# A GLA and retention trunk on one core: values and gates of a retention head as a pair, with seven block products for half their k-tiles

## The chip, the core and the metric

The kernel runs on one core of a Trainium2 chip. The core has TensorE (PE, matrix products into PSUM), VectorE (DVE), ScalarE (ACT), GpSimd (POOL) and SyncE (SP), and 16 DMA engines that SP, ACT and POOL feed through queues. The metric is the device time of one execution in microseconds, as the median of several runs. "PEld" in the profile is the loading of the stationary operand of a matmul, which overlaps the matmuls.

## The reference

Two layers with a residual each, then an RMS norm. The first is gated linear attention (GLA, 4 heads), the second retention (8 heads); both project a normalised input of 256 tokens x 2048 to queries, keys, values and gates, and project 4096 gated outputs back. The retention layer, which the change is about, in short:

```
proj = h @ w_in                                  # h: 256 x 2048
q, k, v, gate = split(proj)                      # per head 256, 256, 512, 512 columns
q, k = rotary(q), rotary(k)
o = (q k^T * decay, causal) v                    # per head
o = (o - mean(o)) * rsqrt(var(o) + EPS) * gn_g + gn_b
h = h + (o * silu(gate)) @ w_out
```

All arrays are float32.

## The kernel before

**Precision.** A float32 operand is split in two parts, hi and lo = x - hi, both of type float32r, and a product is three matmuls: hi·hi, hi·lo and lo·hi. The activations are split once (`xhl` for the layer's input, `ogt` for the gated outputs; 16 k-tiles of 128 rows, 2 parts, 256 tokens). The weights stream from HBM and are split on the way: ScalarE copies a piece to hi (L152), VectorE subtracts to get lo (L153).

**Groups and pieces.** All weights lie in one array, in the order of use, in groups of 2048 x 512. A group is 16 k-tiles; a load (`emit_raw`, L119, SP's queue) brings 4 k-tiles (1 MB), a split piece is 2 k-tiles (128 x 1024). There are three buffers for loads and three for hi and lo; pieces are split up to two ahead of TensorE (`LOOK`). `group_x` (matmuls at L189 to L191 in `mm3`) gives 2 token halves x 512 columns: per piece 12 matmuls of 512 columns. `group_w` (L229 to L233) gives the transposed queries and keys in four PSUM banks.

**A retention head** (`ret_head`) takes three groups: queries and keys (`rqk`), values (`rv`), gates (`rg`). While TensorE runs the `rv` group, `ret_scores` applies the rotation (L812 to L817), splits q and k, multiplies them and the decay table, and splits the scores. In the `rg` group `o_part` multiplies scores and values, takes mean and variance with the batch statistics instructions (L868, L869) and normalises (L870 to L880). The gate product (L890) and the transposes into `ogt` (L459 to L466) run in the next head's `rqk` group. After four heads `out_half` multiplies their 2048 gated columns with `w_out` in four groups and adds to the residual `resid`, which stays in SBUF.

**Order.** These small works are generators in a queue (`side`), of which one step is emitted after each piece; `drain_side` empties it. The tile framework then places each instruction on its engine's queue by priority and by its own estimate of when the inputs are there. Each queue runs in order. SP's queue holds the loads, POOL's the small tables (decay, `gn_g`, `gn_b`).

Of the kernel before, what the change touches and what calls it, by code (L numbers as in the profile page):

```python
# [10 lines left out]
F32 = mybir.dt.float32  # L11
# [6 lines left out]
P = 128  # L18
# [7 lines left out]
CHUNK = 4  # L26
LOOK = 2
DMA_LOOK = 2
# [25 lines left out]

@with_exitstack
def kernel(
# [20 lines left out]
    raw_p = pool("raw", 3)  # L77
    hi_p = pool("hi", 3)
    lo_p = pool("lo", 3)
# [4 lines left out]
    sc_p = pool("sc", 2)  # L84
# [3 lines left out]
    acc_p = pool("acc", 4, space=psum)  # L88
    lev_p = pool("lev", 2, space=psum)
    mis_p = pool("mis", 2, space=psum)  # L90

# [6 lines left out]
    n_groups = w_all.shape[0]  # L98
    raws, splits = {}, {}
    emitted = {"raw": 0, "sub": 0}  # L100
    per_raw = CHUNK // SUB
    raws_per_group = NKT // CHUNK

    last0 = (n_groups - 1) * NSUB

    def emit_raw(parts=1):
        c = emitted["raw"]
        if c >= n_groups * raws_per_group:
            return
        t = raw_p.tile([P, CHUNK, GW], F32, tag="raw", name=f"raw{c}")  # L110
        g, j = divmod(c, raws_per_group)
        src = w_all[g, :, j * CHUNK * GW : (j + 1) * CHUNK * GW].rearrange("p (k n) -> p k n", n=GW)
        step = CHUNK // parts
        raws[c] = t
        emitted["raw"] += 1
# [24 lines left out]
    def emit_split(pieces=1, between=None):  # L140
        i = emitted["sub"]
        if i >= n_groups * NSUB:
            return
        c, j = divmod(i, per_raw)
        while emitted["raw"] <= min(c + DMA_LOOK, n_groups * raws_per_group - 1):
            emit_raw()
        src = raws[c][:, j * SUB : (j + 1) * SUB, :]
# [11 lines left out]
        if j == per_raw - 1:  # L159
            del raws[c]  # L160
        emitted["sub"] += 1

# [16 lines left out]
    def next_weights():  # L179
        i = state["sub"]  # L180
        while emitted["sub"] <= min(i + LOOK, n_groups * NSUB - 1):
            emit_split()
# [10 lines left out]
    def group_x(lhs, name, hook=None, deadline=None, bank=None):  # L193
        bank = bank or (acc_p, "acc")
        ps = [bank[0].tile([P, GW], F32, tag=bank[1], name=f"{name}_ps{t}") for t in range(2)]
        for j in range(NSUB):
# [9 lines left out]
        return ps  # L206

    def group_w(rhs, name, extra=None):
        ps = [acc_p.tile([P, 2, SEQ], F32, tag="acc", name=f"{name}_ps{c}") for c in range(4)]
        for j in range(NSUB):  # L210
# [3 lines left out]
            if last:  # L214
                order = [(q, c) for c in range(4) for q in range(SUB)]
            if j < 3 and extra is not None:
# [28 lines left out]

    def rsqrt(y, m, n, name):
# [17 lines left out]
    resid = const([P, 2, D], "resid")  # L264
# [55 lines left out]
    w0 = emit_raw(4)  # L320
# [3 lines left out]
    w0(2, 2)  # L324
    load_xt(1)(0, 4)
    w1 = emit_raw(2)
    w1(0)
    w1(1)
    load_xt(2)(0, 4)
    emit_raw()  # L330
# [20 lines left out]
    def square_sum(t, c):  # L351
        junk = sg_p.tile([P, GW], F32, tag="sg", name="sqj")
        nc.scalar.activation(
            junk, resid[:, t, c * GW : (c + 1) * GW], AF.Square, accum_out=ssum[:, t, c : c + 1]
# [40 lines left out]
    def gate_low_rank():  # L395
        for t in range(2):
            keep(nc.sync.dma_start(resid[:, t, :], x_n[:, t, :]))
# [42 lines left out]
    def o_mms(sc, v, name):  # L440
        ps = [acc_p.tile([P, GW], F32, tag="acc", name=f"{name}_ps{t}") for t in range(2)]
# [238 lines left out]
    def out_cols(c, ps, t, first, final):  # L680
        dst = resid[:, t, c * GW : (c + 1) * GW]
# [8 lines left out]
    def out_half(first, final, name):  # L690
        for c in range(4):
# [5 lines left out]
            ps = group_x(ogt, f"{name}{c}", deadline=5)  # L697
# [4 lines left out]
            for _ in transpose_out(  # L702
                lambda t, j: resid[:, t, c * GW + j * P : c * GW + (j + 1) * P],
# [16 lines left out]
    def out_tail():  # L720
# [4 lines left out]
        for t in range(2):  # L725
# [3 lines left out]
            ps = [acc_p.tile([P, half], F32, tag="acc", name=f"tail_ps{t}{n}") for n in range(2)]  # L729
# [11 lines left out]
            for n in range(2):  # L741
                dst = resid[:, t, base + n * half : base + (n + 1) * half]
# [8 lines left out]
            for c in (0, 1, 3, 2):  # L751
                src = resid[:, t, c * GW : (c + 1) * GW]
# [53 lines left out]
    def ret_scores(h, box):  # L806
# [207 lines left out]
```

## Time and profile before

| | |
|---|---|
| median of 3 runs | 1416.22 us (1416.16 to 1416.98) |
| profiled execution | 1415.53 us, of it the span 1413.8 us |
| granted TensorE clock | 0.998 |
| busy: PE / DVE / ACT / POOL | 1402.0 / 905.3 / 696.0 / 46.6 us |
| DMA | 266.72 MB, mean 189 GB/s |
| one retention head (start to start of `rqk`) | 70.03 us |

A row by line says: line, engine, operation, output and inputs by the program's names with shape and type, count, then busy time in us and the mean of one in ns, and the idle time of the engine just before, with what ended it. A row of a stretch gives its length and the busy time and count of each engine, the granted clock, the DMA's busy share and GB/s. A row of DMA issues gives count, KB of one and the median us from issue to landing.

### The profile page before, as it was taken

Reading aid. Unit: us, or ns where it says so; the run is one execution under the profiler, and the core shown is the slowest. Engines: PE = TensorE matmul, PEld = TensorE weight load, DVE = VectorE, ACT = ScalarE, POOL = GpSimd, SP = SyncE. Lnnn points to the kernel's source line nnn. Section 1 sums busy time; section 2 is a strip of 40 time slices with the busy share of each in tenths; the row PEclk is TensorE's granted clock in tenths of the full one; section 3 lists DMA queues with packets and bytes.
Section 4 is the critical chain, followed back from the end, with each engine's and each line's share of the span. In section 5 each row is a group of like instructions: output and inputs, shape, how many; then the busy total and the mean of one; then the engine's idle time right before and its main releaser. Section 6 shows DMA issues by size and latency. Waiting matters only on the chain.

```text
span 1413.8 us, 17507 instructions
## 1 busy us (share of the span) xinstructions
PE 1402.0 (99%) x6800; PEld 1179.7 (83%) x6800; DVE 905.3 (64%) x1415; ACT 696.0 (49%) x904; POOL 46.6 (3%) x99
## 2 busy tenths in 40 slices
PE   8999999999999999999999999999999999999997
PEld 7888888888888888888888888888888888888887
DVE  6595795555846774655666666665556666666664
ACT  6665654533555655454444444444344444444453
POOL 1010020000000010000000000000000000000000
PEclk9999999999999999999999999999999999999999
DMA  8654554555555555555555555555555555555662
GB/s 304 242 173 140 208 176 164 195 187 190 177 174 184 182 187 179 179 180 193 193 194 185 199 179 199 181 197 183 204 182 183 197 184 202 180 204 176 207 216 90
DMA packets 40147, 266.72 MB, mean 189 GB/s; under 512 B 4848, under 2 KB 5360, under 8 KB 9344
## 3 DMA queue, kind: packets, MB, share of 16 engines
q1 hardware_dynamic: 36672, 256.92, 53.7%
q0 software_dynamic: 2240, 7.21, 1.5%
q10 hardware_dynamic: 1152, 1.48, 0.3%
q8 instruction: 53, 0.87, 0.2%
q14 instruction: 30, 0.25, 0.0%
HBM read 263.49 MB, written 2.10 MB: 188 GB/s over the span
## 4 chain that ended last, share of the span: by engine, by line
PE 99%; DMA 0%; ACT 0%; DVE 0%; issue 0%; ACTq 0%; DVEq 0%
PE rqk_ps L232 8%; PE gv_ps L189 4%; PE gg_ps L189 4%; PE rv_ps L189 4%; PE gv_ps L191 4%; PE rv_ps L190 4%; PE gg_ps L190 4%; PE gg_ps L191 4%; PE gv_ps L190 4%; PE rv_ps L191 4%; PE rg_ps L189 4%; PE rg_ps L190 4%; PE rg_ps L191 4%; PE rqk_ps L233 4%; PE gqk_ps L232 4%; PE gb_ps L189 2%
## 5 line engine op out<-in xcount | busy, mean ns | idle before, releaser
L153 DVE TENSOR_TENSOR lo<-raw,hi 128x1024 fp32r<-128x1024 f32 (+1 forms) x473 | 576.9, 1222 | 422.1 <-ACT hi L152 421.3
L152 ACT ACTIVATE hi<-raw 128x1024 fp32r<-128x1024 f32 (+1 forms) x473 | 499.3, 1057 | 600.6 <-PE rg_ps L191 104.6
L232 PE MATMUL rqk_ps<-xhl,hi 128*128 128x512 f32 x480 | 166.9, 398 | 0.0
L233 PE MATMUL rqk_ps<-xhl,lo 128*128 128x256 f32 x480 | 126.4, 280 | 0.0
L232 PEld LDWEIGHTS rqk_ps<-xhl,hi 128*128 128x128 f32 x480 | 88.8, 188 | 17.5
L190 PE MATMUL rv_ps<-lo,xhl 128*128 128x512 f32 x256 | 100.4, 392 | 0.0
L190 PE MATMUL gv_ps<-lo,xhl 128*128 128x512 f32 x256 | 100.4, 392 | 0.0
L190 PE MATMUL gg_ps<-lo,xhl 128*128 128x512 f32 x256 | 100.4, 392 | 0.0
L191 PE MATMUL gv_ps<-hi,xhl 128*128 128x512 f32 x256 | 100.2, 392 | 0.0
L191 PE MATMUL gg_ps<-hi,xhl 128*128 128x512 f32 x256 | 100.0, 391 | 0.0
L191 PE MATMUL rv_ps<-hi,xhl 128*128 128x512 f32 x256 | 99.7, 389 | 0.0
L190 PE MATMUL rg_ps<-lo,xhl 128*128 128x512 f32 x256 | 99.6, 389 | 0.0
L191 PE MATMUL rg_ps<-hi,xhl 128*128 128x512 f32 x256 | 99.6, 389 | 0.0
L189 PE MATMUL gv_ps<-hi,xhl 128*128 128x512 f32 x256 | 93.1, 391 | 0.0
L189 PE MATMUL rv_ps<-hi,xhl 128*128 128x512 f32 x256 | 92.1, 390 | 0.0
L233 PEld LDWEIGHTS rqk_ps<-xhl,lo 128*128 128x128 f32 x480 | 89.1, 189 | 3.4
L189 PE MATMUL rg_ps<-hi,xhl 128*128 128x512 f32 x256 | 91.8, 389 | 0.0
L189 PE MATMUL gg_ps<-hi,xhl 128*128 128x512 f32 x256 | 91.7, 391 | 0.0
L232 PE MATMUL gqk_ps<-xhl,hi 128*128 128x512 f32 x216 | 72.7, 397 | 0.0
L191 PEld LDWEIGHTS rv_ps<-hi,xhl 128*128 128x128 f32 x256 | 48.1, 188 | 10.0
L191 PEld LDWEIGHTS rg_ps<-hi,xhl 128*128 128x128 f32 x256 | 48.0, 188 | 10.0
L190 PEld LDWEIGHTS rg_ps<-lo,xhl 128*128 128x128 f32 x256 | 48.1, 188 | 10.0
(273 smaller groups left out, 2402.7 us busy)
## 6 DMA issues: line engine op xcount, KB each, us to landing
raw<-in_w_all SPq DMA_DIRECT2D x238, 1024.0 KB, 4.9
resid<-in_x_n SPq DMA_DIRECT2D x2, 1024.0 KB, 8.1
gg<-in_gn_g POOLq DMA_DIRECT2D x8, 256.0 KB, 3.7
gb<-in_gn_b POOLq DMA_DIRECT2D x8, 256.0 KB, 4.5
raw<-in_w_all SPq DMA_DIRECT2D x3, 512.0 KB, 6.6
xt<-in_x_t SPq DMA_DIRECT2D x3, 512.0 KB, 8.1
dm<-in_dmat POOLq DMA_DIRECT2D x8, 192.0 KB, 2.6
fn<-in_final_norm POOLq DMA_DIRECT2D x4, 256.0 KB, 4.2
```

The lines of the kernel that those rows point to most:

```text
L152: a = nc.scalar.activation(hi[:, sl], src[:, sl], AF.Copy)
L153: b = nc.vector.tensor_tensor(lo[:, sl], src[:, sl], hi[:, sl].bitcast(F32), ALU.subtract)
L189: mm(ps, xh, hi[:, q, :], start=kt == 0, stop=False)
L190: mm(ps, xh, lo[:, q, :], start=False, stop=False)
L191: mm(ps, xl, hi[:, q, :], start=False, stop=kt == NKT - 1)
L232: mm(ps[c], wh, rhs[:, kt, :, :], start=kt == 0, stop=False)
L233: mm(ps[c][:, 0, :], wl, rhs[:, kt, 0, :], start=False, stop=False)
```

## The change

**The pair.** For a retention head write the first 8 k-tiles of the input as four blocks: token halves 1 and 2, k-tiles 0 to 3 (a) and 4 to 7 (b). With the gate weights g and the value weights v, also in halves a and b, the 2 x 2 block product (tokens x {g, v}) takes eight products of 4 k-tiles when written out. The new kernel forms it with seven (`product`), of block sums: X1a·ga, S1·vb, S2·(ga+va), S3·(ga+va+vb), X1b·gb, S4·(va+vb), X2b·(ga+va+vb+gb), where S2 = X2a - X2b or its like are sums of the input blocks (`make_sums`: VectorE and ScalarE once, for all eight heads). K-tiles 8 to 15 go as before (`direct`). A product accumulates in one of the PSUM banks A, B, C, V1, which are partly copied out and partly accumulated on.

**The weight sums.** The pair streams 14 pieces per head from HBM and keeps four of them, x (ga) and z (vb), in their buffers. POOL's queue issues DMAs that add a second piece from HBM onto a buffer (`accum_op`): va onto x, later va onto z and gb onto x. VectorE adds z onto x in place. After each sum the buffer is split again, so the pair takes 22 splits. The order of the pieces is x x, v4, z z, v5, x x, v6, x x, g2 g3, v7, z z, g4, g5, x x, g6, g7 (numbers are pieces of two k-tiles; the doubles serve a product, the others `direct`).

**Streams.** A load is now one piece of 512 KB, into eight buffers assigned ahead (`_plan`); there are four hi and lo buffers, and splits run three pieces ahead.

**The head's rest.** Rotation, scores, outputs and normalisation (`ret_tasks`) now run mostly in the next head: two steps at the head's end, the others in the next `rqk` group and the first pieces of the pair. Mean and variance come from ScalarE's accumulated sums. The `rqk` group uses two of the pair's banks and the two `lev` banks; scores, outputs and transposes share the two `mis` banks. After heads 3 and 7, `out_half` does the first six of eight pieces of its first two groups, beside which the last head's rest runs, and then the last two of each.

**The residual.** `resid` and the sums share one buffer of 16 KB per partition: the residual is stored to HBM (ScalarE's queue) before heads 0 and 4 and loaded in `out_half`; the sums are stored in head 3 and loaded for head 4 (these three from POOL's queue). Heads are counted from 0.

```diff
-CHUNK = 4
-LOOK = 2
-DMA_LOOK = 2
+QK = 4
+LOOK = 3
+DMA_LOOK = 6
+NRAW = 8
...
+    def pair(g, v):
+        x = [load(g, 0), load(g, 1)]
+        for j in range(2):
+            use(x[j], post=[(x[j], (v, j))])
+        plain(v, [4])
+        z = [load(v, 2), load(v, 3)]
+        for j in range(2):
+            use(z[j])
+        plain(v, [5])
+        for j in range(2):
+            use(x[j])
+        plain(v, [6])
+        for j in range(2):
+            use(x[j], pre=z[j], post=[(z[j], (v, j)), (x[j], (g, 2 + j))])
+        plain(g, [2, 3])
+        plain(v, [7])
+        for j in range(2):
+            use(z[j])
+        plain(g, [4, 5])
+        for j in range(2):
+            use(x[j])
+        plain(g, [6, 7])
...
+        for h in range(4 * half, 4 * half + 4):
+            plain(("rqk", h))
+            pair(("rg", h), ("rv", h))
+        out_cols_of("ro", half, CUT)
...
+    def emit_raws(c):
+        while emitted["raw"] < len(loads):
+            n = emitted["raw"]
+            h = held.get(bufs[n])
+            if n > c and (n > c + DMA_LOOK or (h is not None and last_use[h] >= emitted["sub"])):
+                break
+            emit_raw()
...
+        for n in range(i + 1, min(i + 1 + EARLY, len(subs))):
+            at, by = subs[n][:2]
+            if by is not None and n not in added:
+                added.add(n)
+                nc.vector.tensor_tensor(raws[at], raws[at], raws[by], ALU.add)
...
+        for n, key in post:
+            nc.gpsimd.dma_start(raws[n], block(key), accum_op=ALU.add)
+        emit_raws(c)
...
+    def three(ps, xh, xl, hi, lo, q, stop):
+        start, again = id(ps) not in begun, {"skip_group_check": id(ps) in closed}
+        begun.add(id(ps))
+        mm(ps, xh, hi[:, q, :], start=start, stop=False, **again)
+        mm(ps, xh, lo[:, q, :], start=False, stop=False, **again)
+        mm(ps, xl, hi[:, q, :], start=False, stop=stop, **again)
+        if stop:
+            closed.add(id(ps))
+    def product(ps, left, stop=False):
+        for j in range(2):
+            hi, lo = next_weights()
+            for q in range(SUB):
+                k = j * SUB + q
+                three(ps, left(k, 0), left(k, 1), hi, lo, q, stop and k == QK - 1)
+    def direct(lhs, ps, j, stop=False):
+        hi, lo = next_weights()
+        for t in range(2):
+            cols = slice(t * P, (t + 1) * P)
+            for q in range(SUB):
+                kt = j * SUB + q
+                three(ps[t], lhs[:, kt, 0, cols], lhs[:, kt, 1, cols], hi, lo, q, stop and q == SUB - 1)
...
+        s = rs_p.tile([P, 4, QK, 2, P], F32R, tag="rs", name=name)
+        cur["s"] = s
+        tt = nc.vector.tensor_tensor
+        y = [t4_p.tile([P, QK, SEQ], F32, tag="t4", name=f"{name}_y{i}") for i in range(2)]
+        for i in range(2):
+            part = lhs[:, i * QK : (i + 1) * QK].bitcast(F32)
+            tt(y[i], part[:, :, 0, :], part[:, :, 1, :], ALU.add)
+        yield
+        one_, two = slice(0, P), slice(P, SEQ)
+        f = [t4_p.tile([P, 2, QK, P], F32, tag="t4", name=f"{name}_f{i}") for i in range(2)]
+        f3, f5, f6, f7 = f[0][:, 0], f[0][:, 1], f[1][:, 0], f[1][:, 1]
+        tt(f5, y[0][:, :, two], y[1][:, :, two], ALU.subtract)
+        tt(f6, f5, y[0][:, :, one_], ALU.subtract)
+        yield
+        tt(f3, f6, y[1][:, :, one_], ALU.add)
+        tt(f7, y[0][:, :, one_], y[0][:, :, two], ALU.subtract)
+        yield
+        for i, x in ((0, f3), (1, f5), (2, f6), (3, f7)):
+            keep(nc.scalar.activation(s[:, i, :, 0, :], x, AF.Copy))
+            keep(tt(s[:, i, :, 1, :], x, s[:, i, :, 0, :].bitcast(F32), ALU.subtract))
...
+        po = [mis_p.tile([P, GW], F32, tag="mis", name=f"ro{h}_ps{t}") for t in range(2)]
+        o_mms(sc, box["v"], f"ro{h}", po)
+        o = o_p.tile([P, 2, GW], F32, tag="o", name=f"ro{h}")
+        mv = st_p.tile([P, 2, 2], F32, tag="mv", name=f"mv{h}")
+        for t in range(2):
+            nc.scalar.activation(o[:, t, :], po[t], AF.Copy, accum_out=mv[:, 0, t : t + 1])
+        nc.vector.tensor_scalar(mv[:, 0, :], mv[:, 0, :], -1.0 / GW, None, ALU.mult)
+        for t in range(2):
+            mean = mv[:, 0, t : t + 1]
+            nc.scalar.activation(po[t], o[:, t, :], AF.Square, bias=mean, accum_out=mv[:, 1, t : t + 1])
+        yield
+        for t in range(2):
+            keep(nc.vector.scalar_tensor_tensor(o[:, t, :], o[:, t, :], mv[:, 0, t : t + 1], gg, ALU.add, ALU.mult))
...
+        q_ps = [acc(1, f"rqk{h}_ps{c}", (P, 2, SEQ), [c + 2])[0] for c in range(2)]
+        q_ps += [lev_p.tile([P, 2, SEQ], F32, tag="lev", name=f"rqk{h}_ps{c}") for c in (2, 3)]
+        group_w(lhs, f"rqk{h}", lambda j: step() if j < NSUB - 1 else None, q_ps)
...
+        mine = ret_tasks(h, qk, r, r2, {"v": v, "sg": sg})
+        product(A, plain(0, 0), stop=True)
+        step()
+        direct(lhs, (C, V1), 4)
+        copy(sg[:, 0, :], A)
+        step()
+        product(C, summed(0))
+        direct(lhs, (C, V1), 5)
+        while tasks:
+            step()
+        product(B, summed(1), stop=True)
+        direct(lhs, (C, V1), 6)
+        copy(o[:, 1, :], B)
+        begun.discard(id(B))
+        closed.discard(id(B))
+        product(A, summed(2), stop=True)
+        product(B, plain(4, 0))
+        copy(o[:, 0, :], A)
+        direct(lhs, (C, V1), 7, stop=True)
+        tt(o[:, 0, :], o[:, 1, :], o[:, 0, :], ALU.subtract)
+        product(A, summed(3), stop=True)
+        tt(o[:, 0, :], C, o[:, 0, :], ALU.add)
+        copy(sg[:, 1, :], A)
+        direct(lhs, (B, A), 4)
+        v_split(0)
+        tt(o[:, 1, :], o[:, 1, :], sg[:, 1, :], ALU.subtract)
+        direct(lhs, (B, A), 5)
+        tt(o[:, 1, :], V1, o[:, 1, :], ALU.add)
+        product(A, plain(4, 1))
+        v_split(1)
+        tasks.append(mine)
+        direct(lhs, (B, A), 6)
+        step()
+        direct(lhs, (B, A), 7, stop=True)
+        step()
+        for t in range(2):
+            g_done(t)
...
+            if cut and c == 0:
+                if True:
+                    for i in range(2):
+                        pend[i] = acc(2, f"{name}{i}_ps")
+                        steps_x(pend[i], ogt, range(cut), lambda j: hook(i, j))
+                    get_resid(f"{name}_resid")
+                    for i in range(2):
+                        steps_x(pend[i], ogt, range(cut, NSUB))
...
+    put_resid("resid_g")
+    if True:
+        tasks.append(make_sums(xhl, "sums"))
+        for h in range(4):
+            if h == 3:
+                keep_sums("sums")
+            ret_head(h)
+    slots = deque((2, 3, 0, 1))
+    out_half(True, False, "ra", CUT, out_steps)
+    put_resid("resid_r")
+    if True:
+        reload_sums("sums2")
+        for h in range(4, 8):
+            ret_head(h)
+    slots = deque((2, 3, 0, 1))
+    out_half(False, True, "rb", CUT, out_steps)
```

More of the change, by code (lines that the diff above doesn't have):

```diff
@@ L205, in group_x, with group_w @@
             advance()
[L206 to L209 removed]
+    def group_w(rhs, name, extra=None, ps=None):
+        given = ps is not None
+        ps = ps or acc(4, f"{name}_ps", (P, 2, SEQ))
         for j in range(NSUB):
@@ L688, with out_half @@
     fns = {}
-    def out_half(first, final, name):
+    def out_half(first, final, name, cut=0, hook=None):
+        pend = {}
         for c in range(4):
@@ L897, with out_steps @@
+        v_split(1)
[4 more added lines that the diff above has]
+        step()
+        for t in range(2):
+            g_done(t)
+        begun.clear()
+        closed.clear()
+    def out_steps(i, j):
+        step(2 if i == 0 else 1)
     for h in range(2):
```

340 lines of the change are left out of this document (207 added, 133 removed).

## The prediction

> **What bounds the kernel now.** The page comes first (busy time of each engine, chain of work that ended last), then one retention head as a window, then the start times of single matmuls, and last the DMA.
>
> ```profile
> span 1413.8 us, 17507 instructions
> PE 1402.0 (99%) x6800; PEld 1179.7 (83%) x6800; DVE 905.3 (64%) x1415; ACT 696.0 (49%) x904; POOL 46.6 (3%) x99
> PE 99%; DMA 0%; ACT 0%; DVE 0%; issue 0%; ACTq 0%; DVEq 0%
> ```
>
> The chain is TensorE alone. Of the 11.8 us in which it is idle, none lies in a retention head:
>
> ```profile
> core 0: us, PE busy (x) PEld busy (x) DVE busy (x) ACT busy (x) POOL busy (x), PEclk, DMA share, GB/s
> 808.96:878.99 70.03, 70.03 (x349) 59.27 (x348) 46.54 (x67) 31.61 (x40) 1.61 (x3) 1.00 0.57 191
> 808.96:832.20 23.24, 23.24 (x138) 20.38 (x137) 12.97 (x16) 11.22 (x17) 0.00 (x0) 1.00 0.53 181
> 170.00:190.00 20.00, 20.00 (x102) 17.00 (x101) 20.00 (x64) 12.44 (x17) 0.56 (x2) 1.00 0.48 161
> ```
>
> The first row is one whole head (head 2): TensorE 70.03 of 70.03 us. The second is its query/key group. The third is a stretch of a GLA head with VectorE busy for the whole 20 us, and TensorE still without a gap. A busy row can hide waits, because the ends of matmuls are modelled, so the pace is read from starts (start, duration, engine, line):
>
> ```profile
> 832.04 0.39 PE L189 MATMUL rv_ps<-hi,xhl 128*128 128x512 f32 x1
> 832.27 0.39 PE L190 MATMUL rv_ps<-lo,xhl 128*128 128x512 f32 x1
> 832.50 0.39 PE L191 MATMUL rv_ps<-hi,xhl 128*128 128x512 f32 x1
> ...
> 834.77 0.61 PE L189 MATMUL rv_ps<-hi,xhl 128*128 128x512 f32 x2
> ```
>
> The thirteenth starts 834.77 - 832.04 = 2.73 us after the first: 0.227 us each, the same between neighbours, within a bank and across banks. So TensorE is issuing without a gap, and a matmul fewer is 0.227 us less, as long as nothing else comes late.
>
> **What goes.** Before, the first eight k-tiles of values and gates take 8 x 2 token halves x 2 groups x 3 = 96 matmuls of 512 columns per head. Seven products of 4 k-tiles x 3 are 84. The other half (`direct`) keeps its 96; the query/key group, the scores, the outputs and the transposes keep their numbers. 12 matmuls x 0.227 = 2.72 us per head, 21.8 us for eight heads. A head becomes 70.03 - 2.72 = 67.31 us, of which the pair's 180 matmuls are 40.8. This term is certain; all the rest can only add waits, since no other TensorE work goes.
>
> **VectorE and ScalarE.** Rows of head 2, grouped by line (count, then busy us and mean ns):
>
> ```profile
> L153 DVE TENSOR_TENSOR lo<-raw,hi 128x1024 fp32r<-128x1024 f32 x24 | 29.3, 1223 | 18.6 <-ACT hi L152 18.6
> L429 DVE SCALAR_TENSOR_TENSOR rv<-rv_ps,r,rv 128x512 fp32r<-128x512 f32 x2 | 1.4, 751 | 0.4 <-ACT rv L428 0.4
> L868 DVE BATCH_NORM_STATS2 bs<-ro_ps 128x6 f32<-128x512 f32 x2 | 1.4, 700 | 2.5 <-PE ro_ps L450 2.5
> L890 DVE TENSOR_TENSOR ro<-ro,rsg 128x512 f32<-128x512 f32 x2 | 1.4, 692 | 0.4 <-ACT rsg L437 0.4
> L812 DVE TENSOR_TENSOR ra<-rqk,trig 128x1024 f32<-128x1024 f32 x1 | 1.2, 1224 | 0.0
> L813 DVE TENSOR_TENSOR rb<-rqk,trig 128x512 f32<-128x512 f32 x1 | 0.7, 684 | 0.0
> L869 DVE BATCH_NORM_AGGREGATE mv<-bs 128x2 f32<-128x6 f32 x2 | 0.4, 176 | 0.0
> L466 DVE TENSOR_TENSOR ogt<-rot_tp,ogt 128x256 fp32r<-128x256 f32 x4 | 1.6, 416 | 0.0
> ```
>
> The pair splits 22 weight pieces where the two groups split 16, because the x and z pieces are split again after each sum. VectorE: +6 splits x 1.223 = 7.3; +2 adds of 128x1024 as L812, 2.4; +5 combinations of 128x512 as L890, 3.5; +0.2 for the mean; -1.4 and -0.4 for the batch statistics. That is +11.6: 58.2 of 67.3 us, 86%.
>
> ```profile
> L152 ACT ACTIVATE hi<-raw 128x1024 fp32r<-128x1024 f32 x24 | 25.4, 1058 | 33.3 <-PE rg_ps L191 13.1 <-PE rqk_ps L232 9.6 <-PE rv_ps L191 7.7
> L428 ACT ACTIVATE rv<-rv_ps,r 128x512 fp32r<-128x512 f32 x2 | 1.4, 690 | 0.9 <-PE rv_ps L191 0.9
> 837.80 2.35 DVE L153 TENSOR_TENSOR lo<-raw,hi 128x1024 fp32r<-128x1024 f32 x2
> ```
>
> ScalarE: +6 splits x 1.058 = 6.3, +4 PSUM copies and +2 copies and 2 squares of the outputs, 8 x 0.69 = 5.5: 43.4 us, 65%. L152's idle time says that splits now wait for TensorE to free a buffer, so they run as far ahead as the buffers let them.
>
> In the pair alone VectorE has 22 splits (26.9), two adds (2.4), five combinations and two value splits (5.0), rotation L812 and two L813 (2.6), two gate products (1.4) and four of L466 (1.7): 40.0 of 40.8 us as durations. Back to back it is less: two splits take 2.35 us, 1.13 from start to start. A product piece (six matmuls) lasts 1.36 us, so a run of four of them (pieces 10 to 13) can be fed. I cost all this at nothing, covered by TensorE's 40.8 us; the row that bears it out is the window at 170 to 190, VectorE full and TensorE without a gap. If the cover goes, each us of a late split is a us per head, 8 us in all.
>
> One place has little cover. After the sixth product ScalarE copies bank A to sg, and the next direct piece writes B for 1.36 us and then A. A split that has just begun ahead of the copy makes 1.06 + 0.69 = 1.75 us, 0.4 late. Bounds 0 and 0.4 us per head (no gain, a wait only); I take 0.2, because ScalarE is idle for a third of the time.
>
> **The accumulating DMAs.** Six a head, 512 KB each, from POOL's queue. None is in the trace; the nearest rows are plain ones (KB each, us from issue to landing; above them a 2 us slice of a busy stretch):
>
> ```profile
> DMA  9189473039573491780099743692753910891995
> GB/s 385 53 250 391 72 324 143 0 74 406 111 303 164 70 397 57 152 373 0 4 266 307 274 205 98 127 397 33 254 238 66 381 78 0 217 385 61 246 391 84
> raw<-in_w_all SPq DMA_DIRECT2D x14, 1024.0 KB, 4.8
> gg<-in_gn_g POOLq DMA_DIRECT2D x2, 256.0 KB, 3.7
> q1 hardware_dynamic: 36672, 256.92, 53.7%
> mask<-in_mask POOLq DMA_DIRECT2D x1, 256.0 KB, 6.6
> ```
>
> Full slices move about 391 GB/s, so 512 KB are 1.34 us (T) of all engines; gg's 3.7 us less its 0.67 leave 3.0 us fixed on POOL's queue.
>
> When must they land? Take 0 as the start of the pair on TensorE, product pieces 1.36, direct pieces 2.72: piece 7 (x again) starts at 10.9, piece 10 (x with z added) at 16.3, 15 and 16 (z again) at 24.5 and 25.8, 19 (x, the last time) at 32.6. With four buffers the split of piece n starts when piece n-4 ends, and is done 1.06 + 1.22 = 2.3 us later: piece 10's from 10.9 to 13.2. It must start 2.3 us ahead of its matmuls at the latest. The first accumulates (v into x) thus have from about -6.0 (splits start three query/key pieces ahead) to 8.6: 14.6 us. The last (g into x) have 13.2 to 30.3. Tightest is the second z: from 13.2 to 25.8 - 2.3 = 23.5 us, 10.3 us. In program order it is third in POOL's queue, and lands after 3.0 + 3T: at T = 1.34 after 7.0, hidden. It begins to be late at T = 2.4; at 2.7 it is 0.8 us late. Should POOL issue both z first, it is 3.0 + 2T, and in time to T = 3.6.
>
> Ends for T: 1.34 (raw; less isn't possible, the bytes are the same), and from the mask row, as if all beyond 3.0 us were transfer, 2 x 3.6 = 7.2, for which the accumulate is 14 us late. I take 1.34, since raw is the nearest row (same source, rows and target), and 0.1 us per head for queueing behind the raw loads. DMA time in all: 22 plain pieces and 6 accumulates are 28 x 1.34 = 37.5 of 67.3 us.
>
> The Trainium skill speaks against this (Collectives: The Full Stack, "The bandwidth ceiling: the fold count and why AG ≠ RS ≠ AR"): a reducing DMA reads two sources, which halves its rate. No run here shows it; as an estimate from that page T would be 2.7, and the sum 6 us longer at most.
>
> **Moved and added besides.** Raw loads become twice as many of half the size; SP's issues are not on the chain. With x and z held, four of the eight buffers are left for plain pieces, 2 MB ahead: nothing, covered by a piece used per 2 us and a landing of about 3.4 (2.1 fixed, 1.34). The residual goes to HBM and back twice, the sums once, 2 MB each, 5.4 us at 391 GB/s plus 3: the earliest need is 28 us away (first summed product, after the query/key group), so nothing; they queue ahead of the first accumulates on POOL, with slack of the same size. The stores wait on ScalarE's queue for the last residual add; the splits behind are three pieces ahead. The sums of x cost VectorE two 1.22 and eight 0.69, 8 us in the first query/key group, where 23.2 - 13.0 = 10.2 us are free. The head's rest moves past one query/key group: scores and outputs come 30 us later, in time for `out_half`, whose first two column groups do six of eight pieces before they need the last head. The GLA half and the tail change nothing that sets TensorE's pace. All together I take 0.
>
> Sum: median 1416.22 (profiled execution 1415.53, 0.7 below; its span plus 1.7). 1415.53 - 21.8 + 8 x (0.2 + 0.1) = 1396.1, plus 0.7 to the median: **1396.8 us**.
>
> **The rivals.**
> 1. Slower: the accumulates are slow, and the second z holds piece 16. For: nothing in the trace adds in flight, and four of them are issued within about 3 us. Against: a plain transfer has 3 us to spare. It turns at 3.0 + 3T - 10.3 = 2.72, T = 3.3, two and a half times a plain load. At T = 4.0: 4.7 late, 8 x 4.7 = 38 more than 1394.4: 1432. At 7.2: 1508.
> 2. Splits late in the product runs: ScalarE and VectorE queues are in order, a split behind a combination waits 0.7 to 1.2 us, once or twice a head. For: 40.0 of 40.8 us. Against: the window at 170. 1.5 us per head: 1407.
> 3. Nothing gained: TensorE is no longer what ends last, VectorE's 86% or the DMA's is, with waits of about 2.7 us per head: 1416. Against: neither sum comes near 67 us.
>
> **How the numbers follow.** A measurement tells about 0.2%, 2.8 us. Forecast (1393 to 1404) 0.53; rival 2 (1404 to 1413) 0.12; rival 3 0.05; rival 1 0.30, of it 0.13 up to 1432. Faster 0.65, same 0.05, slower 0.30. The range 1392 to 1432 leaves out some 0.18, nearly all of it slow accumulates; the forecast's own is 1393 to 1404.
>
> **What would show it.** Right: 6704 matmuls, TensorE busy near 1380, a head of 67.3 us without idle time, 22 splits and two adds per pair, VectorE near 1005 us in all, accumulates landing in under 7 us, no split waiting for a DMA. Wrong: in the waits, ScalarE's hi or TensorE's re_ps behind a DMA into raw (rival 1); TensorE behind lo with the DMA long landed (rival 2); heads of 70 us.

## The result, and the profile after

The changed kernel takes 1401.87 us (median of 4 runs, 1400.90 to 1402.71); the kernel before, on the same chip, 1416.19 us. The ratio is 0.9898, with a 95% interval from 0.9880 to 0.9915: 14.3 us faster, where 19.4 were forecast. The profiled execution took 1402.71 us, 0.8 above the median; its span is 12.9 us shorter than before. TensorE's work shrank as forecast, so the question is where 7.5 us (8.9 in the profiled execution) of the 21.8 us went that the missing matmuls are worth.

The page of the changed kernel: span, busy time of each engine, and the chain of work that ended last.

```profile
span 1400.9 us, 18373 instructions
PE 1386.3 (99%) x6704; PEld 1161.2 (83%) x6704; DVE 987.1 (70%) x1505; ACT 786.2 (56%) x1052; POOL 87.7 (6%) x151
PE 94%; DMA 3%; DVE 1%; ACT 1%; issue 1%; POOL 0%; ACTq 0%; POOLq 0%; DVEq 0%
```

There are 6704 matmuls, 96 fewer, as counted ahead. The chain is no longer TensorE alone: DMA has 3% of it, where it had 0%. Now by stretches (window, then busy us and count of each engine, clock, DMA share, GB/s). The part ahead of the first retention head, from the start to the first `rqk` matmul, before:

```profile
0.00:668.79 668.79, 665.10 (x3153) 555.50 (x3153) 434.16 (x756) 364.45 (x493) 33.67 (x75) 1.00 0.56 190
```

The changed kernel: that part, then head 1 (to be held against the 70.03 us of a head before), and head 4.

```profile
0.00:673.02 673.02, 668.65 (x3153) 555.71 (x3153) 439.24 (x763) 365.64 (x494) 30.25 (x75) 1.00 0.62 192
734.90:802.30 67.40, 67.40 (x336) 56.93 (x335) 56.83 (x79) 42.72 (x58) 6.92 (x9) 1.00 0.80 233
1031.80:1094.50 62.70, 61.65 (x299) 51.42 (x298) 43.16 (x44) 35.06 (x40) 5.79 (x7) 1.00 0.90 283
```

The first part has the same 3153 matmuls and takes 4.2 us longer. Head 1 is 67.4 us with TensorE busy throughout. Head 4 is shorter because it carries no rest of an earlier head, but it has 1.05 us in which TensorE is idle. From start to start of `rqk`, heads 1, 2, 5 and 6 take 67.45, 67.75, 67.61 and 67.44 us. What TensorE waited for, of more than 0.2 us and beside two waits of the first microseconds (1.9 and 1.8 us, the same in the kernel before; engine and line, what it waited for; us in total, times, longest):

```profile
PE re_ps L362 <- DVE lo L259: 0.8, 1, 0.8
PE ra_ps L296 <- ACT ogt L645: 0.5, 1, 0.5
PE rb_ps L296 <- ACT ogt L645: 0.5, 1, 0.5
PE re_ps L361 <- ACT hi L258: 0.3, 1, 0.3
PE ga_ps L296 <- ACT gsg L617: 0.3, 1, 0.3
```

Each of these rows counts one wait, and the modelled ends of the matmuls hide a part of it. Single matmuls show the whole and the place (start, duration, engine, line; idle time and what ended it in brackets):

```profile
227.42 0.39 PE L298 MATMUL gv_ps<-hi,xhl 128*128 128x512 f32 x1
227.91 0.73 PE L628 MATMUL go_ps<-gv,sc 128*128 128x512 f32 x2
228.69 0.50 PE L296 MATMUL gg_ps<-hi,xhl 128*128 128x512 f32 x1
...
976.31 0.38 PE L639 MATMUL rot_tp<-ident,ro 128*128 128x128 f32 x2
977.24 0.50 PE L296 MATMUL ra_ps<-hi,ogt 128*128 128x512 f32 x1 [0.55 <-ACT ogt L645]
...
1082.71 0.39 PE L363 MATMUL re_ps<-hi,xhl 128*128 128x512 f32 x1
1083.38 0.49 PE L361 MATMUL re_ps<-hi,xhl 128*128 128x512 f32 x1 [0.29 <-ACT hi L258]
1084.64 0.50 PE L362 MATMUL re_ps<-lo,xhl 128*128 128x512 f32 x1 [0.77 <-DVE lo L259]
```

Starts that should lie 0.227 us apart lie 0.49 apart at 227.9, 0.67 at 1083.4 and 1.26 at 1084.6. There are three places: the turn from values to outputs to gates in a GLA head (three times in this trace), the first output group after heads 3 and 7, and one late split in head 4. With the paces beside them they make this account of the profiled execution:

| where | us lost against "21.8 less" |
|---|---|
| ahead of the first retention head, 673.02 - 668.79 | 4.2 |
| head 4, 62.75 against 61.13 where its accumulates are left out (below) | 1.6 |
| head 2, 67.75 against 67.45; head 5, 67.61 against 67.44 | 0.5 |
| `ra` and `rb`, 0.8 each | 1.6 |
| remainder: above all the pace of the heads, 67.45 instead of 67.31 | 1.0 |
| sum: 21.8 - 12.9 | 8.9 |

### The profile page after: what moved, and what is told of

It reads as the page before. It is cut to its first block, busy times and chain, and to the rows that moved or that the text cites. A ratio compares the mean times of both kernels' runs of the same rounds, so it can differ in the third digit from the quotient of the medians.

```text
span 1400.9 us, 18373 instructions
## 1 busy us (share of the span) xinstructions
PE 1386.3 (99%) x6704; PEld 1161.2 (83%) x6704; DVE 987.1 (70%) x1505; ACT 786.2 (56%) x1052; POOL 87.7 (6%) x151
## 3 DMA queue, kind: packets, MB, share of 16 engines
q0 software_dynamic: 9728, 40.77, 13.4%
## 4 chain that ended last, share of the span: by engine, by line
PE 94%; DMA 3%; DVE 1%; ACT 1%; issue 1%; POOL 0%; ACTq 0%; POOLq 0%; DVEq 0%
PE re_ps L362 7%; PE re_ps L363 7%; PE re_ps L361 7%; PE rqk_ps L342 7%; PE gg_ps L296 4%; PE gv_ps L296 4%; PE gv_ps L297 4%; PE gv_ps L298 4%; PE gg_ps L297 4%; PE gg_ps L298 4%; PE gqk_ps L342 4%; PE rqk_ps L343 4%; PE ga_ps L296 2%; PE gb_ps L296 2%; PE ga_ps L298 2%; PE gb_ps L297 2%
## 5 line engine op out<-in xcount | busy, mean ns | idle before, releaser
L259 DVE TENSOR_TENSOR lo<-raw,hi 128x1024 fp32r<-128x1024 f32 (+1 forms) x521 | 632.3, 1221 | 329.5 <-ACT hi L258 325.7
L258 ACT ACTIVATE hi<-raw 128x1024 fp32r<-128x1024 f32 (+1 forms) x521 | 549.3, 1058 | 465.5 <-PE gg_ps L298 61.1
L362 PE MATMUL re_ps<-lo,xhl 128*128 128x512 f32 x352 | 137.4, 390 | 0.8 <-DVE lo L259 0.8
L363 PE MATMUL re_ps<-hi,xhl 128*128 128x512 f32 x352 | 137.0, 389 | 0.0
L343 PE MATMUL rqk_ps<-xhl,lo 128*128 128x256 f32 x480 | 135.4, 282 | 0.0
L361 PE MATMUL re_ps<-hi,xhl 128*128 128x512 f32 x352 | 131.2, 391 | 0.3 <-ACT hi L258 0.3
L362 PEld LDWEIGHTS re_ps<-lo,xhl 128*128 128x128 f32 x352 | 66.1, 188 | 15.8 <-DVE lo L259 2.2
L363 PEld LDWEIGHTS re_ps<-hi,xhl 128*128 128x128 f32 x352 | 66.1, 188 | 13.7
L361 PEld LDWEIGHTS re_ps<-hi,xhl 128*128 128x128 f32 x352 | 65.7, 188 | 13.7 <-ACT hi L258 0.7
L267 POOL DMA_DIRECT2D raw<-in_w_all x48 | 41.7, 876 | 285.0 <-DMA raw<-in_w_all 170.6
L343 PE MATMUL gqk_ps<-xhl,lo 128*128 128x256 f32 x216 | 57.8, 280 | 0.0
L296 PEld LDWEIGHTS gg_ps<-hi,xhl 128*128 128x128 f32 x256 | 48.1, 188 | 10.9 <-DVE gv L609 1.5
```

What stands on the lines that cost most here:

```text
L258: a = nc.scalar.activation(hi[:, sl], src[:, sl], AF.Copy)
L259: b = nc.vector.tensor_tensor(lo[:, sl], src[:, sl], hi[:, sl].bitcast(F32), ALU.subtract)
L267: nc.gpsimd.dma_start(raws[n], block(key), accum_op=ALU.add)
L296: mm(ps, xh, hi[:, q, :], start=kt == 0, stop=False)
L343: mm(ps[c][:, 0, :], wl, rhs[:, kt, 0, :], start=False, stop=False)
L361: mm(ps, xh, hi[:, q, :], start=start, stop=False, **again)
```

## The experiments

All medians are of kernels timed beside the kernel before, which took 1415.6 to 1416.2 us in these comparisons. A ratio is to it, with its 95% interval. Neighbouring intervals overlap, so where two kernels differ by some 2 us the place of the difference is read from the starts of the heads in the traces.

| kernel | median, us | ratio |
|---|---|---|
| the change | 1401.87 | 0.9898 [0.9880, 0.9915] |
| no_products | 1424.21 | 1.0056 [1.0041, 1.0071] |
| overwrite | 1399.67 | 0.9885 [0.9869, 0.9902] |
| no_add | 1399.74 | 0.9887 [0.9872, 0.9902] |
| in_order | 1415.01 | 0.9996 [0.9986, 1.0005] |
| sums_again | 1399.88 | 0.9885 [0.9869, 0.9902] |
| gla_banks | 1398.32 | 0.9875 [0.9860, 0.9890] |
| streams_only | 1417.35 | 1.0010 [1.0000, 1.0020] |
| four_by_dma | 1449.06 | 1.0234 [1.0215, 1.0253] |
| all_three | 1395.84 | 0.9856 [0.9841, 0.9871] |

### Everything of the change but the seven products

```diff
     def pair(g, v):
-        x = [load(g, 0), load(g, 1)]
-        ...
+        plain(v)
+        plain(g)
...
-        product(A, plain(0, 0), stop=True)
-        ...
+        for j in range(NSUB):
+            direct(lhs, (A, B), j, stop=j == NSUB - 1)
...
+        for j in range(NSUB):
+            direct(lhs, (C, V1), j, stop=j == NSUB - 1)
...
```

> The changed kernel with every k-tile of values and gates by plain matmuls again (16 pieces per head instead of 22, no block sums, no accumulating DMAs); the streams, the bank assignment, the head's rest in the next head and the stored residual stay. Theory A (each matmul fewer is worth 0.227 us, the rest of the change costs about 7 us): 96 matmuls more, 1401.9 + 21.8 = 1424, less up to 2 us that head 4 waits for accumulates: 1421 to 1424, slower than the kernel before by 5 to 8 us. Rival B (the products themselves lose a part of their gain to late splits and DMAs, the rest of the change is free): 1416, no difference from the kernel before.

It took 1424.21 us: 22.3 more than the change and 8.0 more than before. So the products, with their sums, splits, accumulates, copies and combinations, bring 22.3 us, and what else was changed costs 8.0. Its first `rqk` matmul comes at 672.84 us, as late as in the change, and its heads take 70.43 us, 0.4 more than before. So most of the loss is beside the products, not in them. (A whole head is 2.98 us longer here than in the change, not the 2.72 us of twelve matmuls; where the other 0.26 us come from is not shown.)

### The accumulates, replaced and left out

```diff
         for n, key in post:
-            nc.gpsimd.dma_start(raws[n], block(key), accum_op=ALU.add)
+            nc.gpsimd.dma_start(raws[n], block(key))
```

> The accumulating DMAs become plain ones of the same pieces from the same queue (they overwrite the buffer instead of adding, so values and gates come out wrong; that part of the computation is left out). Theory A (the accumulates are hidden but for head 4): 1400 to 1402, at most 1.6 us faster than the changed kernel; each transfer lands sooner, by the price of the adding, 512 KB at 391 GB/s, about 1.3 us alone. Rival B (accumulates cost a wait in most heads): 1396 or less.

```diff
-        for n, key in post:
-            nc.gpsimd.dma_start(raws[n], block(key), accum_op=ALU.add)
```

> The six accumulating DMAs per head are left out (the weight sums that they form are missing, so values and gates come out wrong); VectorE's add and all 22 splits stay. Theory A: only head 4's wait of 1.6 us goes, 1400.3 us, and what else the changed kernel has lost against 1394.4 stays. Rival B (the traffic of the accumulates slows the raw loads and so the splits everywhere): 1396 or less.

Both leave weight sums out, so their values and gates are not those of the layer. They took 1399.67 and 1399.74 us, the same. Adding in flight costs the change 2.2 us, and moving the bytes costs nothing. In both kernels all whole heads take 67.45 us and head 4 takes 61.13. These rows are head 1 of overwrite, and its DMA issues (KB each, median us to landing):

```profile
734.90:802.30 67.40, 67.40 (x337) 56.93 (x336) 56.12 (x78) 42.70 (x57) 4.79 (x9) 1.00 0.69 230
raw<-in_w_all POOLq DMA_DIRECT2D x48, 512.0 KB, 4.2
```

The same stretch of no_add:

```profile
734.90:802.30 67.40, 67.40 (x336) 56.92 (x335) 56.13 (x78) 42.70 (x57) 1.63 (x3) 1.00 0.58 182
```

And in the change, all accumulates, then the first two of head 1 alone, which have the queue to themselves:

```profile
raw<-in_w_all POOLq DMA_DIRECT2D x48, 512.0 KB, 8.2
...
raw<-in_w_all POOLq DMA_DIRECT2D x1, 512.0 KB, 5.8
raw<-in_w_all POOLq DMA_DIRECT2D x1, 512.0 KB, 5.5
```

The DMA's share gives the price of one. Six plain transfers raise it from 0.58 to 0.69, which is 0.11 x 67.4 / 6 = 1.24 us of all engines each; six accumulating ones raise it to 0.80, which is 2.5 us each. An accumulate takes the engines twice as long as a plain load. The Trainium skill says of the reducing step of a collective that it needs two source reads and so runs at half the rate of a copy (Collectives: The Full Stack, "The bandwidth ceiling: the fold count and why AG ≠ RS ≠ AR"). The ratio here, 0.22 to 0.11 for an add within one core, agrees. Alone on its queue an accumulate also lands 1.6 to 1.9 us later than the plain one of overwrite (5.8 and 5.5 us against 3.8 and 3.9 for the first two of that head).

### The order of POOL's queue

The change as run issues the two accumulates onto z first and then the two onto x, though the program names them z, x, z, x: the framework placed them by when it expected their inputs. Here they keep the program's order.

```diff
         for n, key in post:
-            nc.gpsimd.dma_start(raws[n], block(key), accum_op=ALU.add)
+            keep(nc.gpsimd.dma_start(raws[n], block(key), accum_op=ALU.add))
```

> The accumulating DMAs are held to program order on GpSimd's queue: z, x, z, x, where the changed kernel's trace shows z, z, x, x. By the prediction's deadline the second z is then third in the queue: it lands 3.0 + 3T us after the first issue against 10.3 us of room. With T of 2.7 (the spacing of landings in a burst is 2.6 to 3.9) it is 0.8 late in each head: 1401.9 + 6 = 1408; with T of 3.5, 3.2 late: up to 1427. If the lookahead of the splits covers more than I think: within 1 us of 1401.9.

It took 1415.01 us: 13.1 more than the change, and no longer to be told from before. The order of four instructions on one queue decides over all but some 1 us of the gain, and the better order was not the program's: the framework chose it. Its heads take 68.7 to 70.2 us. POOL's queue in its head 3 (start, duration; idle time and what ended it), and then ScalarE's:

```profile
915.13 0.87 POOL L267 DMA_DIRECT2D raw<-in_w_all  x1 [4.28 <-DVE raw L253]
918.29 2.67 POOL L267 DMA_DIRECT2D raw<-in_w_all  x3 [2.29 <-DVE lo L259]
```

```profile
923.62 1.07 ACT L258 ACTIVATE hi<-raw 128x1024 fp32r<-128x1024 f32 x1 [0.47 <-PE re_ps L363]
924.59 0.58 ACT L1097 ACTIVATE re<-re_ps 128x512 f32<-128x512 f32 x1
928.61 3.91 ACT L258 ACTIVATE hi<-raw 128x1024 fp32r<-128x1024 f32 x4 [3.44 <-DMA raw<-in_w_all]
```

The first z is issued at 915.13. The first x can't be issued before its own split has been read (the release by `lo`, 2.29 us of idle queue), and the second z stands behind it, third in the queue. It goes out at 918.83 and lands 9.68 us later, at 928.5. ScalarE stands idle for 3.44 us until then, with the split that TensorE needs next. What TensorE waited for, in the whole run:

```profile
PE re_ps L361 <- ACT hi L258: 6.3, 12, 1.1
PE re_ps L362 <- DVE lo L259: 2.5, 8, 0.3
```

In the change the same two rows have 0.3 and 0.8 us, one wait each. The queue there, in head 1, and the landings of its last four issues (7.3, 7.6, 10.4 and 12.6 us after issue):

```profile
774.75 0.87 POOL L267 DMA_DIRECT2D raw<-in_w_all  x1 [4.27 <-DVE raw L253]
777.02 0.86 POOL L267 DMA_DIRECT2D raw<-in_w_all  x1 [1.40 <-ACT ogt L645]
778.11 0.89 POOL L267 DMA_DIRECT2D raw<-in_w_all  x1 [0.23 <-DVE ogt L646]
779.71 0.87 POOL L267 DMA_DIRECT2D raw<-in_w_all  x1 [0.71 <-DVE lo L259]
```

Both z are in place at 784.6, 9.9 us after the first was issued, against 13.4 us in in_order. The slow ones are the two x, and those have time.

### The sums made twice instead of stored and loaded

```diff
         for h in range(4):
-            if h == 3:
-                keep_sums("sums")
             ret_head(h)
...
-        reload_sums("sums2")
+        tasks.append(make_sums(xhl, "sums2"))
```

> The sums of the input blocks are formed a second time ahead of head 4 (VectorE and ScalarE, as ahead of head 0) instead of being stored in head 3 and loaded in head 4. GpSimd's queue then has nothing in front of head 4's first accumulating DMAs that waits for the residual's store. Theory A (that wait in the queue is what held head 4): head 4 from 62.75 to about 61.2 us and head 2 from 67.75 to 67.45, 1401.9 - 1.8 = 1400. Rival (the second accumulates of head 4 are late by the traffic itself): 1401.9 within 0.5; or VectorE's 8 us of sums hold head 4: 1402 to 1404.

It took 1399.88 us, 2.0 less, with heads of 67.45 to 67.51 us and head 4 at 61.49: nearly all that the accumulates cost is gone, though every accumulate is there. So the cost was not theirs alone, but theirs beside the store and the load of the sums. POOL's queue in the change, in head 4:

```profile
1044.90 0.54 POOL L413 DMA_DIRECT2D sums<-sums_kept  x1 [74.67 <-DMA resid_r<-ra_resid]
1048.60 0.89 POOL L267 DMA_DIRECT2D raw<-in_w_all  x1 [3.17 <-DVE lo L259]
1051.43 0.87 POOL L267 DMA_DIRECT2D raw<-in_w_all  x1 [1.93 <-DVE lo L259]
```

The sums and the residual share one buffer, so the load of the sums waits until the store of the residual has landed, and POOL's queue waits with it. But that wait holds no accumulate up: it is over at 1044.90, and the two accumulates wait for `lo` until 16.8 and 19.65 us after the head's start. In sums_again, with nothing ahead of them, they go out at 17.3 and 19.65 us. What differs is the traffic: beside the 2 MB of the sums, which land at 1055.09, the two take 9.5 and 10.7 us to land, in sums_again 6.0 and 7.1. The chain of the changed kernel shows how that reaches TensorE:

```profile
1032.81 11.55 DMA resid_r<-ra_resid
...
1051.43 10.74 DMA raw<-in_w_all
...
1071.43 10.74 DMA raw<-in_w_all
...
1082.27 1.07 ACT hi L258
1083.37 1.24 DVE lo L259
...
1084.64 0.50 PE re_ps L362
```

The store's 11.55 us makes the load of the sums late, and the second accumulate takes 10.74 us beside it and the first. The splits after it are late, and with them the accumulates onto z and a plain load on SP's queue, which go out 0.9 us later after the head's start than in sums_again. That load, issued at 1071.43, takes 10.74 us too, beside the accumulates, and its split is the one that TensorE waits for.

How near this is to being hidden, gla_banks (below) shows, which stores and loads the sums as the change does. There the residual's store took 9.6 us, the load of the sums went out 11.2 us after the head's start instead of 13.1, the two accumulates landed in 7.9 and 8.2 us, and head 4 took 61.13 us without a wait. Its head 2, in which the store of the sums goes out, took 68.75 us, 1.3 too much, where the change has 67.75. There is one trace of each kernel, so how often either wait comes is open.

### The PSUM banks in the GLA half

The change assigns four banks in turn for all output groups. In a GLA head the second gate group then falls on the banks of the value group just before it, and TensorE waits for their copies. Here the outputs and gates are put on the pair that has been free longer, and the third column group of the second half's output on the two `lev` banks.

```diff
-            po = o_mms(hw["sc"], vs[gi], f"go{g}")
+            which = [2, 3] if gi == 0 and h > 0 else [0, 1]
+            po = o_mms(hw["sc"], vs[gi], f"go{g}", acc(2, f"go{g}_ps", which=which))
...
-            sgs.append(g_evac(group_x(xhl, f"gg{g}", g_hook), r, f"gsg{g}"))
+            pg = acc(2, f"gg{g}_ps", which=[2, 3])
...
+            sgs.append(g_evac(group_x(xhl, f"gg{g}", g_hook, ps=pg), r, f"gsg{g}"))
...
```

> The changed kernel with other PSUM banks in the GLA heads: the second gate group takes the banks of the score products of the first values instead of the second value group's, and the third column group of the GLA output takes the two lev banks. Theory A (the gate group waits for the copies of the values because the four banks are now assigned in turn): the three waits of about 0.7 us go, 1401.9 - 2.1 = 1399.8. Rival (they come from the splits running three ahead, or from smaller loads): no change.

It took 1398.32 us, 3.6 less. The part ahead of the first retention head:

```profile
0.00:669.04 669.04, 665.50 (x3153) 555.41 (x3153) 442.17 (x763) 366.56 (x494) 29.94 (x75) 1.00 0.63 193
```

All the waits at the turn from values to gates are gone, and so is the one of 0.41 us at 253.5, which I had not put down to the banks. Five other kernels that left the GLA half as in the change reached that matmul at 671.83 to 672.25 us (overwrite, no_add, in_order, sums_again, four_by_dma), and a sixth, no_products, at 672.84 us. The change and no_products are late from the start: their first value group begins 1.26 and 0.98 us later than before, that of overwrite 0.14. So of the 4.2 us some 1.0 belong to the one profiled execution (its first matmuls), some 3.0 to the banks, and 0.25 remain. The rest of the 3.6 us isn't the banks': head 4 has no wait here and head 2 a longer one, as said above.

### The streams alone, in the kernel before

```diff
-CHUNK = 4
-LOOK = 2
-DMA_LOOK = 2
+CHUNK = 2
+LOOK = 3
+DMA_LOOK = 6
...
-    raw_p = pool("raw", 3)
-    hi_p = pool("hi", 3)
-    lo_p = pool("lo", 3)
+    raw_p = pool("raw", 8)
+    hi_p = pool("hi", 4)
+    lo_p = pool("lo", 4)
...
```

> The kernel before with nothing but the change's streams: loads of 512 KB two k-tiles at a time, eight buffers for them, three pieces of look-ahead, four hi/lo buffers, one scratch buffer less; no pair, no product blocks, the output groups and the order of the banks as before. Theory A (the 3 us that the change loses ahead of the first retention head come from the order of the PSUM banks in the GLA half, not from the larger loads and smaller buffers): as before, 1416 within 1 us, first matmul of the first retention head within 1 us of 668.8 us after the start. Rival (the larger loads come later, or the scratch buffer is missed): 1418 to 1420, with that matmul at 671 to 673.

It took 1417.35 us, 1.8 more, between the two expectations. The place decides: its first `rqk` matmul comes at 669.09 us, 0.3 later than before, so the GLA loss isn't the streams'. What it loses is in the heads, 0.2 us each (70.21 against 70.02), without a wait of TensorE that the trace shows; the 128 matmuls of `rqk` take 22.73 us from start to start instead of 22.51. Half of the 0.4 us that a head of no_products is longer is this. Why they are slower wasn't found.

### The fourth sum by DMA as well

```diff
         for j in range(2):
-            use(x[j])
+            use(x[j], post=[(x[j], (v, 2 + j))])
         plain(v, [6])
         for j in range(2):
-            use(x[j], pre=z[j], post=[(z[j], (v, j)), (x[j], (g, 2 + j))])
+            use(x[j], post=[(z[j], (v, j)), (x[j], (g, 2 + j))])
```

> VectorE's add of z onto x in each pair is replaced by a fourth accumulating DMA (vb from HBM onto x, issued after x's second split). The room is from piece 7's split to piece 10's, 7.7 to 14.0 us after the pair's start, 6.3 us. An accumulate alone took 5.4 to 5.9 us from issue to landing and 3.1 us more for a second in the queue: the second x lands at about 16.5 against 15.4, 1.1 us late in each head, and the z accumulates queue behind. Theory A: 1401.9 + 9 = 1411, up to 1420. Rival (VectorE was near its limit, and its 2.4 us per head back are worth more): 1400 or less.

It took 1449.06 us, 47.2 more than the change and 2.3% more than before. I had the direction, but not the size (1411, at most 1420). The trace shows why: once VectorE no longer reads z, its accumulates are free to go first, and they do. POOL's queue in head 1, and then the chain there:

```profile
769.29 1.89 POOL L267 DMA_DIRECT2D raw<-in_w_all  x2 [5.00 <-DVE rh_nw L433]
773.10 0.57 POOL L1010 DMA_DIRECT2D gg<-in_gn_g  x1 [1.92 <-DVE ro L1056]
774.83 0.86 POOL L267 DMA_DIRECT2D raw<-in_w_all  x1 [1.16 <-DVE lo L259]
```

```profile
774.83 11.22 DMA raw<-in_w_all
786.16 1.06 ACT hi L258
787.25 1.24 DVE lo L259
788.53 0.79 PE re_ps L362
```

The x that is needed next is issued 5.5 us after two z that have time, and takes 11.22 us beside them. Its way to TensorE is on the chain link by link.

That is not the whole of the 7.9 us that head 1 is longer. After the wait the granted clock (the third number from the end of the row below) is half:

```profile
788.50:794.00 5.50, 5.47 (x13) 4.25 (x14) 4.93 (x8) 5.30 (x8) 1.71 (x2) 0.50 0.70 112
```

The matmuls there start 0.43 us apart (789.12, 789.55, 789.97) instead of 0.227. Of the 7.9 us some 5.0 are the wait and some 2.9 this clock. Heads 1, 2, 5, 6 and 7 have such a stretch, of 3.4 to 6.8 us, and lose 6.2 to 7.9 us; heads 0, 3 and 4 have none and lose 4.5. A slow accumulate costs that much when it is the next thing needed, and nothing when it is not.

### The three repairs together

`sums_again`, `gla_banks`, and a third output group that does its first six pieces before the last head is needed:

```diff
-                for c in range(2):
+                for c in range(3):
...
-                    for i in range(2):
-                        pend[i] = acc(2, f"{name}{i}_ps")
+                    for i in range(3):
+                        if i == 2:
+                            pend[i] = [lev_p.tile([P, GW], F32, tag="lev", name=f"{name}{i}_ps{t}") for t in range(2)]
+                        else:
+                            pend[i] = acc(2, f"{name}{i}_ps")
                         steps_x(pend[i], ogt, range(cut), lambda j: hook(i, j))
                     get_resid(f"{name}_resid")
-                    for i in range(2):
+                    for i in range(3):
                         steps_x(pend[i], ogt, range(cut, NSUB))
...
```

> Three repairs together: sums formed again, other GLA banks, and the output groups of the retention halves taken three instead of two at a time for their first six pieces (the third in the lev banks), which gives the last head's rest 16 us more. Theory A (the losses are separate waits): 1401.9 - 1.8 - 2.1 - 1.6 = 1396.4. Rival (they cover one another or move): 1399 or more.

It took 1395.84 us (1395.53 to 1396.31): 6.0 less than the change, and faster than both kernels. Three of its heads take 67.45 us and one 67.51. The stretch from head 3's start to head 4's, which holds the first output groups, is 160.92 us instead of 161.73, which gives the 0.8 us of `ra` alone. Of the waits of TensorE only those of the first microseconds and one of 0.2 us are left in the list of waits; by the starts of the matmuls this one, a split in head 4, comes 0.3 us late.

## Why the prediction was right, and where it was wrong

The sum was 1396.8 us and the time is 1401.87, inside the range and its own narrower one; the direction and the main term were right. Point by point:

- **12 matmuls fewer, 2.72 us a head.** Right. 6704 matmuls; TensorE busy 1386.3 us, somewhat over "near 1380"; no_products puts the worth of the products at 22.3 us against 21.8, which agrees better than it should: a whole head without them is 2.98 us longer, not 2.72, and the 2.2 us that the accumulates cost count against it. A whole head is 67.45 us, 0.14 over: the pair's 180 matmuls take 41.0 us instead of 40.8, and `rqk` is slower as in streams_only.
- **VectorE and ScalarE covered.** Right. They are busy for 56.8 and 42.7 us of head 1, against 58.2 and 43.4 written; VectorE 987 us in all, where 1005 were written. The 48 more splits are there, 521 against 473. Rival 2 (late splits in the product runs) and rival 3 (VectorE or DMA as the bound) did not happen: with the accumulates out of the way the heads run at 67.45 us with no wait.
- **Bank A, 0.2 us a head.** Not there; no such wait is in the trace. 1.6 us too much.
- **The accumulates.** The step "I take 1.34, since raw is the nearest row" failed: the engines spend 2.5 us on one, the double, and the landing is 5.4 to 15.9 us over the run, not under 7. The estimate from the Trainium skill that stood beside it (T of 2.7, from two source reads) was the nearer value. That the forecast held all the same was luck: the sum took the program's order, and the framework happened to place the other one, which the text allowed for ("should POOL issue both z first"), with time to T = 3.6. In program order, where the second z is late from T = 2.4, in_order measures 13.1 us: that is the mechanism of rival 1, at its place. It ends at no gain rather than slower, since 13.1 us are 1.6 a head, less than the 2.72 at its turning point (T = 3.3). What the working lacked is that an accumulate must also wait for the splits that read its buffer: in in_order the second z was issued 3.7 us after the first.
- **"They queue ahead of the first accumulates on POOL, with slack of the same size."** This failed in head 4. The load of the sums waits for the store of the residual out of the same buffer, 11.55 us, and then moves 2 MB beside the accumulates. The working priced each transfer alone (5.4 us plus 3), and not the store and the load one after the other (11.55 and 10.2 us), nor what the load does to the accumulates beside it, which then land after 9.5 and 10.7 us. Their issue was not held up: what failed is the overlap, not the queue's order. It cost 1.6 us there and, by the 2 MB store, 0.3 in head 2; sums_again gives 2.0 back.
- **"The GLA half and the tail change nothing that sets TensorE's pace."** This is the step that was most wrong: some 3 us. The text counted work, and there is no more of it; what changed is which PSUM bank comes next, and that turned a copy that had time into one that TensorE waits for.
- **"In time for `out_half`".** Wrong by 0.8 us each time: two groups of six pieces don't quite cover the last head's rest, and the first matmul on it waits for ScalarE's `ogt` copy. A third group covers it.

Against the 1396.1 us written for a profiled execution, then: +4.2 ahead of the first retention head (3.0 of it the banks, 1.0 this one execution's start), +1.6 (output groups), +1.3 (2.1 in heads 4, 2 and 5, less the 0.8 allowed for accumulates), -1.6 (bank A), +1.0 (pace). That makes 1402.6; it took 1402.71. What stays open is the pace of `rqk` and of the pair, some 0.14 us a head.

## What to carry to other kernels

When a change takes work off the bound engine, look for the loss in what was moved without adding work: the order of buffers or PSUM banks, each DMA that stands in a queue ahead of something urgent, and each large one that a wait pushes into the time of something urgent. A slow transfer costs nothing or nearly the whole gain depending on its place, so write down for each one by when it is needed and what may go ahead of it or beside it, and settle the good order in the program rather than leave it to the scheduler. Price an operation that the trace lacks by what it must do, not by the nearest row that does less: an add in flight cost the engines twice the plain transfer. After a wait of TensorE, look at the granted clock before putting the whole loss down to the wait.

## What the runs showed of the hardware

- An accumulating DMA from HBM into SBUF occupies the 16 engines for 2.5 us per 512 KB, a plain one for 1.24 us (shares of 0.80, 0.69 and 0.58 above). Its issue holds POOL for 0.86 us, the plain one for 0.53. In overwrite:

```profile
773.51 0.53 POOL L267 DMA_DIRECT2D raw<-in_w_all  x1 [4.32 <-DVE raw L253]
```

- Accumulates slow the plain loads beside them. From 750 to 790 us of the change, where six are issued, ten loads on SP's queue took 8.1 us to land; eleven in the same stretch of overwrite, where the six are plain, took 4.3 us (first the change, then overwrite):

```profile
raw<-in_w_all SPq DMA_DIRECT2D x10, 512.0 KB, 8.1
...
raw<-in_w_all SPq DMA_DIRECT2D x11, 512.0 KB, 4.3
```

- The same accumulates cost 2.2 us, 15 us or 49 us in all, measured against leaving them out, in three orders of one queue (the change, in_order, and four_by_dma, which has two more a head and loses a part by the clock).
- The granted clock fell to 0.50 in five heads of four_by_dma, for 3.4 to 6.8 us, and the matmuls then started 0.43 us apart instead of 0.227. In these heads the longest gap between two starts of matmuls is 1.9 to 4.4 us, in the three without it 1.4 to 1.8 us. Several gaps follow each other there, so no limit can be read from this.
